# A two-layer decoder trunk in float32: values kept in PSUM banks and worked on in place, the softmax divided on ScalarE, other chain rates

## The chip, the core and the metric

The kernel runs on one NeuronCore of a Trainium2 chip. The metric is the device time of one execution in microseconds (us), as the median of several runs: before the change 2885.41 us over three runs (2882.80, 2885.41 and 2891.74).

Five engines work side by side, each through its own instructions in order: TensorE (PE in the profile; its weight loads are PEld), VectorE (DVE), ScalarE (ACT), GpSimd (POOL) and SyncE (SP, which here only issues DMAs). Matmuls read SBUF and write PSUM banks of 128 x 512 float32 values. VectorE and ScalarE read and write both SBUF and PSUM; GpSimd works on SBUF here.

## The reference, cut to what matters

Sequence 1024, width 1024, two layers. `rmsnorm`, `layernorm` and `silu` are the usual ones.

```
for i in range(2):
    a = rmsnorm(h);  u = a @ w_in[i]                    # 2128 columns, split among:
    # q, k, v (8 heads of 64, 2 kv heads), indexer qi (16 heads of 64), ki, wi, conv input, pool input
    idx = sum over 16 heads of relu(qi_h . ki) * wi_h    # causal; the 256 largest keys per query are kept
    y_attn = softmax(q . k / 8 over the kept keys) @ v
    y_conv = silu(layernorm(causal depthwise conv of width 31 (a * sigmoid(g)))) @ conv_pw
    y_pool = (trailing means over 2/4/8/16 positions - x) @ pool_w * pool_scale
    h = h + rmsnorm(concat(y_attn, y_conv, y_pool) @ w_out[i])
    h = h + rmsnorm(square(relu(rmsnorm(h) @ w_up[i])) @ w_down[i])      # 1024 -> 4096 -> 1024
    h = h + sigmoid(h @ ple_gate[i]) * (p[i] @ ple_proj[i])
```

## The kernel before, in words

**Tiles.** Activations are kept transposed (channels on partitions) and the sequence is cut into two halves of 512 positions. Every dense product is a sum of three matmuls of 128 x 512: both operands are split into a high and a low part of a shorter format, and high x high, high x low and low x high are added in one PSUM bank (`dense`, lines L243 to L249). One *unit* (`unit`) is one output tile of 128 x 512 from eight input tiles: 24 matmuls. Its weights are split on the fly in `prepare`: ScalarE makes the high part (L204, `whi`), GpSimd the low part (L205, `wlo`), twice per unit. `split` (L260, L261) and `split_g` (L265, L266) split activations: ScalarE writes the high part, VectorE the difference.

**Stages.** `PHASES` names eight stages of (layer, half). A `win` stage runs the 21 units of the `w_in` product (names M0, M1, MK, I0 to I7, V, Q0 to Q2 for the attention part, A, G, P for convolution and pooling); an `m` stage runs the 8 units of `w_out`, a norm with part of the per-layer embedding, 64 units of up and down projection, a second norm and the 8 units of the gate. By the DMAs of the weights they start at these times of the trace: `win` of layer 0 at 2.1 us (both halves, one behind the other), `m` of layer 0, first half, at 307.1; `win` of layer 1, first half, at 976.2; `m` of layer 0, second half, at 1124.2; `win` of layer 1, second half, at 1647.3; `m` of layer 1, first half, at 1785.4; `m` of layer 1, second half, at 2395.3 up to the end.

**The chain.** Convolution, pooling and attention of a (layer, half) form a second stream of work, written as generators (`conv_pool`, `attention`). Attention has four parts: `index` (scores of 16 heads, ReLU, weighted sum), `select` (the 256th largest value by bisection, 31 passes of counting, then the ties), `softmax` and `weighted` (transposes and the product with v). Each generator yields an estimate of its own cost. `run` puts it between the units: after each unit the chain may spend the unit's cost times the stage's rate in `RATES`. `drain` runs what is left of a (layer, half) before its `m` stage. So `RATES` decides beside which units each part of the chain stands; the order of the instructions on each engine is then made by the scheduler of the tile framework from this program.

**Buffers.** PSUM has 8 banks here: three of ring `pd` for the units and five of ring `bank` for the chain. `dtmp`, `row`, `ctmp`, `cmat` and `slot` are SBUF tiles. `yT` is the running output tile row in SBUF, `rb` the norm factor. A bank is taken when a product is begun (`pd.get`, `banks.get`) and can be written again when the last instruction that reads it has ended (`put`).

**What is touched.** `Sq.add` (L279, L283) squares a tile on ScalarE into a `dtmp` tile and adds it to a sum on VectorE; `evac` (L341) multiplies a bank by `rb` into a `dtmp` tile, which `put` then splits and stores; `index` (L632, L636, L638) evaluates ReLU from a bank into an SBUF row and adds the weighted row; `softmax` (L759 to L769) adds the mask and takes the maximum, exponentiates on ScalarE, and divides on VectorE; the up projection (L969, L971) and the gate (L1006, L1008, L1010) work on `dtmp` tiles.

## Time and profile before

| | us |
|---|---|
| median of three runs | 2885.41 |
| lowest, highest run | 2882.80, 2891.74 |
| the profiled execution | 2882.24 |
| its span, first to last instruction | 2880.4 |
| TensorE busy | 2736.7 (95%) |
| TensorE weight loads | 2250.3 (78%) |
| VectorE busy | 1917.1 (67%) |
| ScalarE busy | 1477.3 (51%) |
| GpSimd busy | 1468.7 (51%) |
| TensorE clock granted, mean over the span | 0.980 |

Busy time is the share of the span in which an engine has an instruction in work. Matmuls overlap in TensorE's pipeline, so the sum of their durations is larger than its busy time. The granted clock is given as a share of full speed: 1.00 is 2.4 GHz, 0.50 is 1.2 GHz, and other values are means over stretches at the two levels. The span can be cut into stretches (a view by windows); a wait is idle time of an engine that ended when another engine's instruction ended, and it is put down to that one.

### The profile page before, as it was taken

How to read it: one execution, taken by the hardware profiler on the slowest of the kernel's cores; microseconds unless marked ns; L12 is line 12 of the kernel's file. 1: busy time of each engine (PE TensorE's matmuls, PEld its weight loads, DVE VectorE, ACT ScalarE, POOL GpSimd, SP SyncE). 2: the span in 40 equal slices, each digit the busy share in tenths (PEclk: the TensorE clock that was granted, in tenths of full speed). 3: DMA queues.
4: the chain of work that ended last, by engine and by line, in shares of the span. 5: the costliest groups of instructions: out<-in, count | busy, mean ns of one | idle time of the engine just before them, and what ended most of it. 6: DMA issues, size and time to landing. Idle time of an engine off the chain costs nothing.

```text
span 2880.4 us, 37724 instructions
## 1 busy us (share of the span) xinstructions
PE 2736.7 (95%) x12648; PEld 2250.3 (78%) x12648; DVE 1917.1 (67%) x3473; ACT 1477.3 (51%) x2804; POOL 1468.7 (51%) x1161
## 2 busy tenths in 40 slices
PE   7889999999998899999999989999999999999998
PEld 6677877787887677778888767878878878788886
DVE  7989779899768877896312558699996662511123
ACT  5356567774553423675434423677744644533343
POOL 4655435444333766554444775455443346544446
PEclk9999999999998999999999999999999999999999
DMA  5676564332433456633323457544223344432233
GB/s 186 194 194 204 161 154 115 100 101 85 103 94 119 158 160 214 187 116 106 98 98 113 136 181 224 149 123 114 93 87 98 104 147 153 147 103 95 95 110 124
DMA packets 195667, 384.91 MB, mean 134 GB/s; under 512 B 17424, under 2 KB 76944, under 8 KB 195472
## 3 DMA queue, kind: packets, MB, share of 16 engines
q1 hardware_dynamic: 138192, 330.58, 35.1%
q0 software_dynamic: 57280, 51.91, 8.7%
q8 instruction: 100, 1.64, 0.2%
q14 instruction: 95, 0.78, 0.1%
HBM read 307.97 MB, written 74.45 MB: 133 GB/s over the span
## 4 chain that ended last, share of the span: by engine, by line
PE 68%; DVE 17%; DMA 6%; issue 4%; POOL 2%; ACT 2%; SPq 0%; POOLq 0%; ACTq 0%; DVEq 0%
PE pd L243 19%; PE pd L249 19%; PE pd L248 19%; PE bank L591 5%; DVE bank L527 3%; PE bank L781 2%; DVE idx L638 2%; POOL wlo L205 1%; DVE dtmp L261 1%; PE bank L790 1%; PE bank L789 1%; DVE slot L266 1%; DMA wraw<-win 1%; DVE dtmp L867 1%; DMA row<-cpS 1%
## 5 line engine op out<-in xcount | busy, mean ns | idle before, releaser
L205 POOL TENSOR_TENSOR wlo<-wraw,whi 128x512 fp32r<-128x512 f32 x824 | 1130.8, 1378 | 1151.0 <-ACT whi L204 1101.2
L243 PE MATMUL pd<-slot,whi 128*128 128x512 f32 x3296 | 1310.4, 398 | 55.3 <-ACT slot L260 11.5
L248 PE MATMUL pd<-slot,whi 128*128 128x512 f32 x3168 | 1248.1, 394 | 4.3 <-DVE slot L266 3.2
L249 PE MATMUL pd<-slot,wlo 128*128 128x512 f32 x3168 | 1242.6, 394 | 3.7 <-POOL wlo L205 3.4
L204 ACT ACTIVATE whi<-wraw 128x512 fp32r<-128x512 f32 x824 | 511.1, 627 | 717.0 <-PE pd L248 494.1
L243 PEld LDWEIGHTS pd<-slot,whi 128*128 128x128 f32 x3296 | 628.4, 191 | 197.1 <-ACT whi L204 18.8
L249 PEld LDWEIGHTS pd<-slot,wlo 128*128 128x128 f32 x3168 | 601.0, 190 | 129.7 <-POOL wlo L205 7.8
L248 PEld LDWEIGHTS pd<-slot,whi 128*128 128x128 f32 x3168 | 602.0, 190 | 126.7 <-DVE slot L266 5.8
L591 PE MATMUL bank<-kd,qst 128*128 128x512 f32 (+3 forms) x1024 | 249.2, 362 | 24.4 <-DVE mxc L759 10.9
L591 PEld LDWEIGHTS bank<-kd,qst 128*128 128x128 f32 x1024 | 181.6, 193 | 57.5 <-DVE mxc L759 12.8
L969 DVE SCALAR_TENSOR_TENSOR dtmp<-pd,rb 128x512 f32<-128x512 f32 x112 | 76.8, 686 | 199.9 <-PE pd L249 199.9
L985 DVE TENSOR_TENSOR yT<-yT,pd 128x512 f32<-128x512 f32 x96 | 65.7, 685 | 197.2 <-PE pd L249 196.9
L638 DVE SCALAR_TENSOR_TENSOR idx<-row,wiT,idx 128x640 f32<-128x640 f32 (+3 forms) x120 | 164.2, 1369 | 20.0 <-ACT row L632 16.0
L261 DVE TENSOR_TENSOR slot<-dtmp,slot 128x512 fp32r<-128x512 f32 x144 | 118.2, 825 | 72.5 <-ACT slot L260 72.2
L527 DVE SCALAR_TENSOR_TENSOR bank<-row,vec,bank 128x512 f32<-128x512 f32 x232 | 163.4, 745 | 0.6
L632 ACT ACTIVATE row<-bank 128x512 f32<-128x512 f32 (+3 forms) x256 | 120.4, 522 | 51.0 <-PE bank L591 39.0
L661 DVE TENSOR_SCALAR_CACHE_REDUCE row<-row,cc 128x640 f32<-128x640 uint16 (+1 forms) x124 | 133.6, 1077 | 16.5 <-ACT row L675 14.6
L283 DVE TENSOR_TENSOR dtmp<-dtmp,dtmp 128x512 f32<-128x512 f32 x100 | 105.0, 1050 | 50.5 <-ACT dtmp L279 49.5
L675 ACT ACTIVATE row<-row,cc 128x768 f32<-128x768 uint16 (+1 forms) x124 | 121.6, 983 | 25.2 <-DVE cc L681 17.5
L971 ACT ACTIVATE dtmp<-dtmp 128x512 f32<-128x512 f32 x128 | 80.1, 629 | 86.6 <-DVE dtmp L969 84.5
L261 DVE TENSOR_TENSOR cmat<-bank,cmat 128x512 fp32r<-128x512 f32 (+1 forms) x160 | 98.3, 630 | 31.1 <-ACT cmat L260 22.3
L759 DVE CUSTOM_DVE_ANT_0 row<-bank,idx 128x512 f32<-128x512 f32 (+3 forms) x160 | 90.8, 591 | 33.1 <-PE bank L591 28.6
(211 smaller groups left out, 2925.0 us busy)
## 6 DMA issues: line engine op xcount, KB each, us to landing
wraw<-wup SPq DMA_DIRECT2D x128, 512.0 KB, 3.2
wraw<-wdown SPq DMA_DIRECT2D x128, 512.0 KB, 3.2
wraw<-win SPq DMA_DIRECT2D x84, 512.0 KB, 4.1
qiS<-dtmp SPq DMA_DIRECT2D x64, 256.0 KB, 2.5
slot<-mixS POOLq DMA_DIRECT2D x32, 512.0 KB, 7.6
wraw<-wgate SPq DMA_DIRECT2D x32, 512.0 KB, 3.4
qst<-qiS POOLq DMA_DIRECT2D x48, 256.0 KB, 4.4
hS<-yT SPq DMA_DIRECT2D x48, 256.0 KB, 2.4
```

Source lines behind the costliest of these rows:

```text
L204: sc.activation(hi, r, AF.Copy)
L205: gp.tensor_tensor(lo, r, hi.bitcast(F32), op=OP.subtract)
L243: te.matmul(ps, wh, xh, start=i == 0, stop=False)
L248: te.matmul(ps, wh, xl, start=False, stop=False)
L249: te.matmul(ps, wl, xh, start=False, stop=i == n - 1)
L261: ve.tensor_tensor(lo, src, hi.bitcast(F32), op=OP.subtract)
L527: ve.scalar_tensor_tensor(acc[:, c] if k == TAPS - 1 else pa, src, w, pa, op0=OP.mult, op1=OP.add)
L591: te.matmul(ps[:, :n1 - n0], q, kd[:, k, k0 + n0:k0 + n1], start=k == 0, stop=k == 1)
L632: sc.activation(r[:, n0:n1], ps[:, :n1 - n0], AF.Relu)
L638: ve.scalar_tensor_tensor(idx[j], r, w, idx[j], op0=OP.mult, op1=OP.add)
L661: ve.tensor_scalar(flags[:, :Ws[j]], of[j], t, None, op0=op, op1=OP.add, accum_out=dst[:, j:j + 1])
L675: sc.activation(flags[:, :Ws[j]], of[j], AF.Sign, scale=-1.0, bias=c[:, j:j + 1], accum_out=cnt[:, j:j + 1])
```

## The change

Six edits, and one table of numbers:

- `Sq.add` takes a bank: the square is written into the bank in place of a `dtmp` tile, except where the tile is kept (the first, and the last where `apart`). In `m` stages the callers hand over the unit's own bank; where the row of `yT` is copied out of it, that copy now stands ahead of the square.
- `scaled` multiplies a bank by `rb` in place, for MK, I2 to I7, Q0 to Q2 and the G columns; `put` then splits out of the bank, which is given back after the split.
- In `index`, ReLU is done in place in the bank, and VectorE adds each piece of up to 512 columns from its bank: two instructions for a head of more than 512 keys, where one stood.
- In `softmax`, ScalarE multiplies by the reciprocal (a Copy with a scale per partition) where VectorE did.
- In the up projection ReLU and norm factor, square and split work in the bank; in the gate, tanh works in the bank and the product with the embedding is written over the embedding's tile.
- `put` no longer gives the source tile back; its callers do.
- `RATES` has other values for six of the eight stages.

```diff
--- before
+++ after
@@ -34,3 +34,3 @@
 
-RATES = (1.2, 1.193, 0.65, 0.823, 0.722, 0.567, 0.768, 0.919)
+RATES = (1.171, 1.114, 0.558, 0.766, 0.722, 0.567, 0.741, 0.946)
 
@@ -276,6 +276,8 @@
 
-        def add(self, src):
-            s = dtmp.get()
+        def add(self, src, bank=None):
+
+            keep = self.n == 0 or self.apart and self.n == NK - 1
+            s = dtmp.get() if keep or bank is None else bank
             sc.activation(s, src, AF.Square)
-            if self.n == 0 or self.apart and self.n == NK - 1:
+            if keep:
                 self.acc.append(s)
@@ -283,3 +285,4 @@
                 ve.tensor_tensor(self.acc[0], self.acc[0], s, op=OP.add)
-                dtmp.put(s)
+                if bank is None:
+                    dtmp.put(s)
             self.n += 1
@@ -343,2 +346,7 @@
 
+        def scaled(ps):
+
+            ve.tensor_tensor(ps, ps, rb, op=OP.mult)
+            return ps
+
         def put(x, parts):
@@ -350,3 +358,3 @@
                     sy.dma_start(dst[k, r0:r0 + b - a, ts], y[a:b])
-            dtmp.put(hi, lo, x)
+            dtmp.put(hi, lo)
 
@@ -379,3 +387,3 @@
                 c = int(name[1])
-                g = evac(ps)
+                g = scaled(ps)
                 sc.activation(g, g, AF.Tanh, scale=0.5)
@@ -384,3 +392,3 @@
                 sy.dma_start(cpS[l, c * P:(c + 1) * P, ts], y)
-                dtmp.put(g, y)
+                dtmp.put(y)
             elif kind == "P":
@@ -409,2 +417,3 @@
                 put(e, [(96, 112, kS[l], 176)])
+                dtmp.put(a, d, e)
             elif name == "I1":
@@ -413,6 +422,7 @@
                 put(d, [(0, P, qiS, P)])
+                dtmp.put(a, d)
             elif name == "MK":
-                put(evac(ps), [(0, P, kS[l], 48)])
+                put(scaled(ps), [(0, P, kS[l], 48)])
             elif kind == "I":
-                put(evac(ps), [(0, P, qiS, P * int(name[1]))])
+                put(scaled(ps), [(0, P, qiS, P * int(name[1]))])
                 if name == "I7":
@@ -420,3 +430,3 @@
             elif kind == "Q":
-                put(evac(ps), [(0, P, qS, P + P * int(name[1]))])
+                put(scaled(ps), [(0, P, qS, P + P * int(name[1]))])
                 if name == "Q2":
@@ -628,13 +638,11 @@
                         q = load_q(qiS, b, h, 16)
-                    t = spare.get()
-                    r = t[:, :W]
+                    w = wiT[:, l, b, h:h + 1]
                     for n0, n1, ps in scores(q[:, h % 4], W, 0):
-                        sc.activation(r[:, n0:n1], ps[:, :n1 - n0], AF.Relu)
+                        r, at = ps[:, :n1 - n0], idx[j][:, n0:n1]
+                        sc.activation(r, r, AF.Relu)
+                        if h == 0:
+                            ve.tensor_scalar(at, r, w, None, op0=OP.mult)
+                        else:
+                            ve.scalar_tensor_tensor(at, r, w, at, op0=OP.mult, op1=OP.add)
                         banks.put(ps)
-                    w = wiT[:, l, b, h:h + 1]
-                    if h == 0:
-                        ve.tensor_scalar(idx[j], r, w, None, op0=OP.mult)
-                    else:
-                        ve.scalar_tensor_tensor(idx[j], r, w, idx[j], op0=OP.mult, op1=OP.add)
-                    spare.put(t)
                     if h % 4 == 3:
@@ -768,3 +776,3 @@
                 ve.reciprocal(ri, rs)
-                ve.tensor_scalar(s, s, ri, None, op0=OP.mult)
+                sc.activation(s, s, AF.Copy, scale=ri)
                 out.append(t)
@@ -939,7 +947,7 @@
                 ve.tensor_tensor(yT[:, o], yT[:, o], ps, op=OP.add)
-                sq.add(yT[:, o])
+                sq.add(yT[:, o], ps)
             else:
                 ps = unit(xs)
-                sq.add(ps)
                 sc.activation(yT[:, o], ps, AF.Copy)
+                sq.add(ps, ps)
             pd.put(ps)
@@ -963,2 +971,3 @@
                     rb = rms_sb(sq)
+                m = slots.get()
                 if early:
@@ -966,10 +975,11 @@
                     ve.tensor_tensor(t, t, rb, op=OP.mult)
+                    sc.activation(t, t, AF.Square)
+                    split(m[:, 0], m[:, 1], t)
+                    dtmp.put(t)
                 else:
-                    ps, t = unit(xs), dtmp.get()
-                    ve.scalar_tensor_tensor(t, ps, 0.0, rb, op0=OP.max, op1=OP.mult)
+                    ps = unit(xs)
+                    ve.scalar_tensor_tensor(ps, ps, 0.0, rb, op0=OP.max, op1=OP.mult)
+                    sc.activation(ps, ps, AF.Square)
+                    split(m[:, 0], m[:, 1], ps)
                     pd.put(ps)
-                sc.activation(t, t, AF.Square)
-                m = slots.get()
-                split(m[:, 0], m[:, 1], t)
-                dtmp.put(t)
                 ms.append(m)
@@ -985,5 +995,5 @@
                     ve.tensor_tensor(yT[:, o], yT[:, o], ps, op=OP.add)
+                if gr == 3:
+                    sqy.add(yT[:, o], ps)
                 pd.put(ps)
-                if gr == 3:
-                    sqy.add(yT[:, o])
                 yield 5.2
@@ -1004,9 +1014,7 @@
             ps = unit(xs, o < 2)
-            th = dtmp.get()
-            sc.activation(th, ps, AF.Tanh, scale=0.5)
-            pd.put(ps)
-            ve.scalar_tensor_tensor(th, th, 1.0, e, op0=OP.add, op1=OP.mult)
+            sc.activation(ps, ps, AF.Tanh, scale=0.5)
+            ve.scalar_tensor_tensor(e, ps, 1.0, e, op0=OP.add, op1=OP.mult)
             y = yT[:, o]
-            gp.tensor_tensor(y, y, th, op=OP.add)
-            dtmp.put(e, th)
+            gp.tensor_tensor(y, y, e, op=OP.add)
+            dtmp.put(e)
             if last:
@@ -1015,3 +1023,3 @@
                 sy.dma_start(hS[o * P:(o + 1) * P, ts], y)
-                nsq.add(y)
+                nsq.add(y, ps)
                 if o == NK - 1:
@@ -1023,2 +1031,3 @@
                     split_g(x[:, 0], x[:, 1], yT[:, j], vec[:, l + 1, V_MIX_PRE + j:V_MIX_PRE + j + 1])
+            pd.put(ps)
             yield 6.5
```

On VectorE, while the index of layer 0, second half, is computed beside the first norm of the `m` stage (`idx_132` is the index of the seventh block of 128 queries, 896 keys wide; L283 and L285 add squares), before and now:

```order
L638 SCALAR_TENSOR_TENSOR idx_132<-row_127,wiT,idx_132 128x896
L283 TENSOR_TENSOR dtmp_104<-dtmp_104,dtmp_102 128x512
L638 SCALAR_TENSOR_TENSOR idx_132<-row_123,wiT,idx_132 128x896
L283 TENSOR_TENSOR dtmp_104<-dtmp_104,dtmp_101 128x512
L638 SCALAR_TENSOR_TENSOR idx_132<-row_125,wiT,idx_132 128x896
L283 TENSOR_TENSOR dtmp_104<-dtmp_104,dtmp_105 128x512
L638 SCALAR_TENSOR_TENSOR idx_132<-row_126,wiT,idx_132 128x896
```

```order
L646 SCALAR_TENSOR_TENSOR idx_132<-bank_141,wiT,idx_132 128x512
L285 TENSOR_TENSOR dtmp_109<-dtmp_109,dtmp_103 128x512
L646 SCALAR_TENSOR_TENSOR idx_132<-bank_144,wiT,idx_132 128x384
L285 TENSOR_TENSOR dtmp_109<-dtmp_109,dtmp_102 128x512
L646 SCALAR_TENSOR_TENSOR idx_132<-bank_143,wiT,idx_132 128x512
L646 SCALAR_TENSOR_TENSOR idx_132<-bank_140,wiT,idx_132 128x384
L646 SCALAR_TENSOR_TENSOR idx_132<-bank_142,wiT,idx_132 128x512
L646 SCALAR_TENSOR_TENSOR idx_132<-bank_141,wiT,idx_132 128x384
```

A head of 896 keys was one instruction that read an SBUF row; it is now a piece of 512 and a piece of 384, each out of a bank. The additions of squares between them come from `post_norm`, which hands no bank to `Sq.add`; they stay as they were.

On VectorE at the gate of layer 0, first half (L1008 and L1016 are the gate's product with the embedding), before and now:

```order
L527 SCALAR_TENSOR_TENSOR bank_143<-row_125,vec,bank_143 128x512
L1008 SCALAR_TENSOR_TENSOR dtmp_104<-dtmp_104,dtmp_108 128x512
L527 SCALAR_TENSOR_TENSOR bank_140<-row_125,vec,bank_140 128x512
L527 SCALAR_TENSOR_TENSOR bank_143<-row_125,vec,bank_143 128x512
L1008 SCALAR_TENSOR_TENSOR dtmp_102<-dtmp_102,dtmp_110 128x512
L527 SCALAR_TENSOR_TENSOR bank_140<-row_125,vec,bank_140 128x512
L527 SCALAR_TENSOR_TENSOR bank_143<-row_125,vec,bank_143 128x512
L527 SCALAR_TENSOR_TENSOR bank_140<-row_125,vec,bank_140 128x512
L266 SCALAR_TENSOR_TENSOR slot_79<-yT,vec,slot_79 128x512
```

```order
L767 ISA row_127,mxc_1404<-bank_140,idx_133 128x512
L767 ISA mxc_1404 128x1
L771 TENSOR_SCALAR nmc_1408<-mxc_1404 128x1
L1016 SCALAR_TENSOR_TENSOR dtmp_103<-pd_137,dtmp_103 128x512
L776 RECIPROCAL ric_1416<-rsc_1412 128x1
L1016 SCALAR_TENSOR_TENSOR dtmp_102<-pd_138,dtmp_102 128x512
L261 TENSOR_TENSOR cmat_122<-bank_141,cmat_121 128x512
L261 TENSOR_TENSOR cmat_118<-bank_144,cmat_117 128x512
L261 TENSOR_TENSOR cmat_120<-bank_143,cmat_119 128x512
```

The taps of the second half's convolution (L527) stood between the gate's instructions; now the last heads of that half's attention stand there (L767 mask and maximum, L776 reciprocal, L261 with `cmat` the split of transposed weights), and the convolution comes later, beside the next `win` stage.

On VectorE in the down projections of layer 0, second half (L985 and L995 add a unit to `yT`), before and now:

```order
L985 TENSOR_TENSOR yT<-yT,pd_137 128x512
L985 TENSOR_TENSOR yT<-yT,pd_138 128x512
L985 TENSOR_TENSOR yT<-yT,pd_139 128x512
L985 TENSOR_TENSOR yT<-yT,pd_137 128x512
L985 TENSOR_TENSOR yT<-yT,pd_138 128x512
L985 TENSOR_TENSOR yT<-yT,pd_139 128x512
```

```order
L537 SCALAR_TENSOR_TENSOR bank_144<-row_123,vec,bank_144 128x512
L537 SCALAR_TENSOR_TENSOR bank_143<-row_123,vec,bank_143 128x512
L509 TENSOR_TENSOR ctmp_116<-row_127,row_126 64x16 x2
L537 SCALAR_TENSOR_TENSOR bank_144<-row_123,vec,bank_144 128x512
L995 TENSOR_TENSOR yT<-yT,pd_139 128x512
L537 SCALAR_TENSOR_TENSOR bank_143<-row_123,vec,bank_143 128x512
L537 SCALAR_TENSOR_TENSOR bank_144<-row_123,vec,bank_144 128x512
L261 TENSOR_TENSOR cmat_120<-ctmp_116,cmat_119 128x512
L537 SCALAR_TENSOR_TENSOR bank_143<-row_123,vec,bank_143 128x512
L537 SCALAR_TENSOR_TENSOR bank_144<-row_123,vec,bank_144 128x512
L266 SCALAR_TENSOR_TENSOR ctmp_115<-bank_140,vec,ctmp_114 128x512
```

The convolution of layer 1, first half (L537 taps, L510 pooling), which stood in the `win` stage of its own layer, now stands here, among units that had nothing of the chain beside them.

## Rows read from the trace of the kernel before

**Rows 1.** The page: the span, and busy time, share and instructions of each engine.

```profile
span 2880.4 us, 37724 instructions
...
PE 2736.7 (95%) x12648; PEld 2250.3 (78%) x12648; DVE 1917.1 (67%) x3473; ACT 1477.3 (51%) x2804; POOL 1468.7 (51%) x1161
```

**Rows 2.** View by windows: stretch, its length, busy time of each engine, granted clock.

```profile
core 0: us, PE busy (x) PEld busy (x) DVE busy (x) ACT busy (x) POOL busy (x), PEclk, DMA share, GB/s
54.00:144.00 90.00, 76.23 (x315) 60.19 (x314) 87.64 (x118) 32.18 (x55) 55.42 (x43) 0.95 0.62 196
432.00:516.00 84.00, 78.11 (x350) 63.15 (x348) 83.38 (x78) 58.86 (x116) 48.40 (x35) 1.00 0.48 119
640.00:684.00 44.00, 37.38 (x157) 30.50 (x156) 43.16 (x66) 16.43 (x31) 19.02 (x14) 0.92 0.26 84
897.00:1010.00 113.00, 95.84 (x389) 74.37 (x387) 97.94 (x122) 41.54 (x73) 66.20 (x51) 0.86 0.46 146
1036.00:1124.00 88.00, 77.69 (x327) 61.32 (x326) 81.53 (x110) 25.57 (x45) 56.60 (x45) 0.94 0.62 198
1368.00:1512.00 144.00, 144.00 (x665) 120.02 (x665) 40.70 (x79) 55.04 (x95) 63.34 (x50) 1.00 0.30 98
1584.00:1656.00 72.00, 68.62 (x304) 54.36 (x303) 41.55 (x41) 32.52 (x57) 51.00 (x35) 1.00 0.41 137
1656.00:1785.00 129.00, 114.92 (x489) 91.33 (x487) 95.07 (x117) 39.02 (x68) 82.33 (x67) 0.96 0.65 201
1872.00:1926.00 54.00, 47.84 (x223) 38.72 (x222) 52.30 (x47) 39.28 (x80) 31.51 (x23) 1.00 0.47 139
2096.00:2142.00 46.00, 41.58 (x183) 33.85 (x182) 45.05 (x70) 17.94 (x34) 20.62 (x14) 0.96 0.27 86
2304.00:2376.00 72.00, 66.34 (x341) 55.23 (x340) 43.67 (x75) 32.09 (x56) 35.01 (x29) 0.95 0.47 147
```

**Rows 3.** By source line: duration in ns, least, median and most, of two forms.

```profile
L283 DVE TENSOR_TENSOR dtmp<-dtmp,dtmp x100: 674/990/2978, 10.0 to 2811.8; 128x512 f32<-128x512 f32 x100
...
L985 DVE TENSOR_TENSOR yT<-yT,pd x96: 671/686/690, 620.2 to 2815.9; 128x512 f32<-128x512 f32 x96
```

**Rows 4.** Groups of VectorE by form: count, busy us, mean ns, idle before, releaser.

```profile
L261 DVE TENSOR_TENSOR slot<-dtmp,slot 128x512 fp32r<-128x512 f32 x144 | 118.2, 825 | 72.5 <-ACT slot L260 72.2
L283 DVE TENSOR_TENSOR dtmp<-dtmp,dtmp 128x512 f32<-128x512 f32 x100 | 105.0, 1050 | 50.5 <-ACT dtmp L279 49.5
...
L867 DVE SCALAR_TENSOR_TENSOR dtmp<-yT,vec,pd 128x512 f32<-128x512 f32 x64 | 46.6, 738 | 16.9 <-PE pd L300 13.8 <-POOL yT L868 2.9
L261 DVE TENSOR_TENSOR dtmp<-dtmp,dtmp 128x512 fp32r<-128x512 f32 x48 | 44.9, 938 | 2.4 <-ACT dtmp L260 2.3
...
L1008 DVE SCALAR_TENSOR_TENSOR dtmp<-dtmp,dtmp 128x512 f32<-128x512 f32 x32 | 38.7, 1212 | 54.8 <-ACT dtmp L1006 54.8
...
L759 DVE CUSTOM_DVE_ANT_0 row<-bank,idx 128x128 f32<-128x128 f32 x16 | 4.5, 283 | 3.6 <-PE bank L591 3.6
```

**Rows 5.** Groups by line, forms together: the index's sums, the softmax on both engines.

```profile
L638 DVE SCALAR_TENSOR_TENSOR idx<-row,wiT,idx 128x640 f32<-128x640 f32 (+3 forms) x120 | 164.2, 1369 | 20.0 <-ACT row L632 16.0
...
L767 ACT ACTIVATE row<-row,nmc 128x384 f32<-128x384 f32 (+5 forms) x96 | 84.3, 878 | 41.4 <-DVE nmc L763 34.1 <-DVE nmc L765 6.9
...
L769 DVE TENSOR_SCALAR row<-row,ric 128x384 f32<-128x384 f32 (+5 forms) x96 | 67.7, 706 | 2.8
...
L638 DVE SCALAR_TENSOR_TENSOR idx<-idx,wiT,idx 128x384 f32<-128x384 f32 (+1 forms) x60 | 54.8, 913 | 14.9 <-ACT idx L632 10.7 <-DVE idx L638 0.5
...
L769 DVE TENSOR_SCALAR ctmp<-ctmp,ric 128x128 f32<-128x128 f32 (+1 forms) x32 | 13.1, 413 | 0.2
```

**Rows 6.** Waits of TensorE from 640 to 684 us: total, times, longest.

```profile
PE bank L591 <- DVE mxc L759: 6.6, 1, 6.6
```

**Rows 7.** Timeline of ScalarE and VectorE at the gate: start, us, instruction, idle before.

```profile
1645.06 0.58 ACT L1006 ACTIVATE dtmp<-pd 128x512 f32<-128x512 f32 x1
...
1651.97 1.10 DVE L283 TENSOR_TENSOR dtmp<-dtmp,dtmp 128x512 f32<-128x512 f32 x1 [1.84 <-ACT dtmp L279]
```

## The prediction

> **What bounds the kernel now.** The page comes first [rows 1]: TensorE is busy for 2736.7 of 2880.4 us, so 143.7 us is all the time in which it does nothing, and no other engine is busy for more than 67% of the span. The view by windows comes second [rows 2]: it shows where those 143.7 us lie. In stretches with little beside the units TensorE is never idle: in 1368 to 1512 it is busy for 144.00 of 144.00 us at a granted clock of 1.00, while VectorE works for 40.70 us. It idles where VectorE is full: 13.77 us of 90 with VectorE busy for 87.64, 17.16 of 113 with 97.94, 5.89 of 84 with 83.38. In most of these stretches the granted clock is below 1.00 as well; a mean of 0.86 over 113 us is 15.8 us of full-speed time that TensorE did not get, because after an idle time part of the stretch ran at 1.2 GHz and not at 2.4. I call idle time plus that deficit the *pot* of a stretch: it is what the stretch could give back at the most.
>
> | stretch | what stands there | idle + deficit = pot, us |
> |---|---|---|
> | 54-144, 1036-1124, 1656-1785 | `win` stages with a convolution | 18.3 + 15.6 + 19.2 = 53.1 |
> | 897-1010 | second norm and gate of layer 0, first half, with a convolution | 17.2 + 15.8 = 33.0 |
> | 640-684, 2096-2142 | end of `select`, first scores after it | 10.1 + 6.3 = 16.4 |
> | 432-516, 1872-1926 | index of the wide blocks beside the first norm | 5.9 + 6.2 = 12.1 |
>
> The third view is by line [rows 3, 4]. A VectorE operation on two SBUF tiles of 512 columns takes 674 ns at the least, 990 in the median and up to 2978 (L283), and 1050 in the mean; with one operand in PSUM it takes 671 to 690 ns, every time (L985). So a PSUM operand buys no faster best case: it takes away a spread that comes only with two SBUF operands.
>
> **VectorE's work, part by part.** I price an operation with a PSUM operand at 686 ns [rows 3]; with a scale per partition at 738, as L867 has it [rows 4]; and narrow pieces by the line from 686 at 512 columns to 283 at 128 (L759), with the same 52 ns on top.
> - Squares: `Sq.add` with a bank covers 24 additions after `w_out`, 24 after the last down projection and 12 at the gates: 60 x (1050 - 686) = 21.8 us. The other 40 have no bank and stay.
> - Up projection: 112 subtractions 825 to 686: 15.6 us. Stored columns of the `win` stages: 40 subtractions 938 to 686: 10.1 us. Gate: 32 products 1212 to 686: 16.8 us.
> - Softmax: 67.7 + 13.1 = 80.8 us leave VectorE [rows 5]. ScalarE gets as many Copies; their form is not in the trace, and the exponentials of the same shapes (878 ns x 96 = 84.3 us for the long rows) bound them from above at about 100 us in all, 0 from below. ScalarE is busy for 51%, so I cost this at nothing where units fill TensorE; where a chain tail is run without cover, each head's division takes up to 0.17 us longer (878 against 706 ns).
> - Index: 180 instructions took 164.2 + 54.8 = 219.0 us [rows 5]. Now each width is cut at 512: the six widths cost 604, 738, 1073, 1207, 1342 and 1476 ns, times 30 = 193 us, a gain of 26. It is all in the widest blocks and in those that were held up; blocks of 640 and 768 keys gain nothing.
>
> Sum: 21.8 + 15.6 + 10.1 + 16.8 + 80.8 + 26 = 171 us of VectorE's 1917, 9%. Most of that lies where TensorE waits for nobody, so it isn't the answer; the pots are.
>
> [...]
>
> **What of it lies on the path.**
> - *Gate, 897-1010.* VectorE's order shows the convolution gone from here. What remains is like 1584-1656, the same place without a chain (pot 3.4), or like 2304-2376, the same place with an attention tail beside it (5.7 + 3.6 = 9.3) [rows 2], and about 5 us for the start of the next `win` stage. The order puts an attention tail there, so about 14 of 33.0 remain: 19 gained, bounds 6 and 25.
> - *Win stages, 53.1.* Each has ten stored columns whose subtraction gets 0.25 us shorter while VectorE is full: about 2.5 us each. Against it a `pd` bank is now held until after the split, at least 0.58 us of ScalarE and 0.69 of VectorE more [rows 3, 7], and three banks turn. Net 7 gained, bounds -7 and 15.
> - *End of select, 16.4.* TensorE's one wait of 6.6 us for the first masked maximum [rows 6] is a queue of tie-breaking work on VectorE that isn't touched; only what stands between it gets lighter. 4 gained, bounds -8 and 12.
> - *Index beside the norm, 12.1.* Half of the waits there are for the norm itself, which isn't touched. 5 gained, bounds -4 and 9.
>
> Against these 35 us stand four costs, with the cover that each has:
> - The convolution of layer 1, first half, moves in among down projections where TensorE had no idle time at all [rows 2]. VectorE has 103 of 144 us free there, enough for 62 taps at 738 ns (46 us), so the taps cost nothing; its small dense products and token sums must still wait for their splits on an in-order TensorE. 3 us, bounds 0 and 10.
> - Banks held longer at the gate. In the trace the way from tanh to the added square is 1645.06 to 1653.07, 8.0 us [rows 7]; the bank is now held over all of it, where 0.6 us did. Two units on the other two banks cover 10.4 us (2 x 24 matmuls at 144.00 us / 665 = 0.217 us, [rows 2]). It is hidden with 2 us to spare; 2 us for the units that come in pairs, bounds 0 and 16 (1 us for each of 16).
> - The last square after `w_out` now follows the copy of the same bank: 0.6 us at each of three norms, 2 us.
> - The lower rates of `m` stages let an attention tail reach into a norm or a gate: 2 us, bounds 0 and 8.
>
> Sum: 19 + 7 + 4 + 5 - 3 - 2 - 2 - 2 = 26 us. The profiled execution took 2882.2 us, 1.8 over its span; that is 3.2 under the median of the runs and inside their spread. 2882.2 - 26 = 2856.2, and on the footing of the median 2859.
>
> **The rivals.**
> - *Relief spreads.* With 171 us off VectorE its queue no longer runs late, TensorE doesn't fall idle, and the clock stays at 2.4 GHz: half of all pots (114.6 us) come back with no cost that shows, 57 us, so 2828. For it: the deficits are nearly as large as the idle times, and a stretch that never idles has none. Against it: several of these waits are for ScalarE, GpSimd or a norm's chain of small steps.
> - *The waits stay.* TensorE idles because its own order is fixed by the scheduler and each wait is a latency (split, norm, tie-breaking), not VectorE's load; what the gate gains is spent in the convolution's new place. 2885. For it: in 640-684 one wait of 6.6 us is two thirds of the pot. [...]
> - *Banks run out, slower.* In the index a bank was free after ReLU (about 0.6 us); now it waits for VectorE too, 0.74 us for its own piece and as much for the one before it. Wide heads take two banks each, so five banks hold two and a half heads, and TensorE's scores stand in order ahead of its units. Once VectorE is more than five pieces (3.7 us) late, each further piece holds up the units behind it. VectorE is busy for 83.38 of 84 us there [rows 2]. If half of the 256 wide pieces of both layers cost 0.35 us each, that is 45 us: 2904. Against it: 26 us less work in just that place, and no two SBUF operands to be held up.
>
> **How the numbers follow.** Forecast 45%, relief spreads 22%, waits stay 18%, banks run out 15%. Within 0.3% of 2885.4 (2876.8 to 2894.1) is what a measurement of this kernel can't tell from no change. The forecast's own range is 2838 to 2880; all but a fifteenth of it counts as faster. Faster: 0.42 + 0.22 + 0.03 of the third case, 0.67. Within: 0.03 + 0.14, 0.17 in all. Slower: 0.15 and a little of the third, 0.16. The range that holds 8 in 10 reaches from "relief spreads", less 14 us that the gate and the `win` stages have left to their upper bounds, 2814, to where "banks run out" begins, 2892.
>
> **What would show it.** Right: no L537 beside the gate of layer 0, first half, and a pot there below 20 us; additions of squares and subtractions at 670 to 690 ns without a tail; VectorE near 1750 us; TensorE's waits for `DVE` in the `win` stages shorter. Wrong: TensorE waits for VectorE's index rows (`idx`) at the scores, more than a few us in all, or for the squares at the gate; or idle time of TensorE above 143 us in all. If TensorE's idle time falls by far more than 26 us, the first rival is right; if it falls only in 897-1010, the second is close.

## The result, and the profile after

The changed kernel takes 2842.68 us (median of four runs, 2840.33 to 2843.85), the kernel before in the same session 2884.11: a ratio of 0.9854 with a 95% interval of 0.9829 to 0.9878, 41.4 us less. The forecast was 2859 with its own range of 2838 to 2880: the time lies in that range, 16 us below the forecast. The profiled execution took 2843.85 us. The page of after, span and busy time, against [rows 1]:

```profile
span 2842.1 us, 37724 instructions
...
PE 2720.5 (96%) x12648; PEld 2242.8 (79%) x12648; DVE 1747.6 (61%) x3473; ACT 1548.1 (54%) x2932; POOL 1418.0 (50%) x1161
```

TensorE's idle time fell from 143.7 to 121.6 us, its mean granted clock rose from 0.980 to 0.985, which is a deficit of (1 - 0.985) x 2842 = 42.6 us in place of 57.6. Together that is 37 us of the 38.3 by which the span is shorter. So nearly all of the gain is idle time and clock, and the pots are the right thing to look at. They are bounds and not exact shares: idle time at a low clock counts twice in a pot, and since the view gives the clock in two digits, the pot of a stage of some 380 us is known to about 2 us. VectorE is busy for 169.5 us less; 171 were worked out.

The durations, after, by line and form (instruction, its operands, count | busy us, mean ns | idle before), against [rows 4, 5]; the first two are those of the source lines with least/median/most in ns, against [rows 3]:

```profile
L285 DVE TENSOR_TENSOR dtmp<-dtmp,pd x60: 672/686/689, 401.6 to 2773.0; 128x512 f32<-128x512 f32 x60
L285 DVE TENSOR_TENSOR dtmp<-dtmp,dtmp x40: 666/684/3155, 8.8 to 2442.5; 128x512 f32<-128x512 f32 x40
```

```profile
L261 DVE TENSOR_TENSOR slot<-pd,slot 128x512 fp32r<-128x512 f32 x112 | 76.6, 685 | 51.3 <-ACT slot L260 51.1
...
L261 DVE TENSOR_TENSOR dtmp<-pd,dtmp 128x512 fp32r<-128x512 f32 x40 | 27.3, 682 | 7.4 <-ACT dtmp L260 7.3
...
L1016 DVE SCALAR_TENSOR_TENSOR dtmp<-pd,dtmp 128x512 f32<-128x512 f32 x32 | 22.0, 690 | 64.8 <-ACT pd L1015 59.8 <-DMA outT<-yT 4.9
```

```profile
L646 DVE SCALAR_TENSOR_TENSOR idx<-bank,wiT,idx 128x512 f32<-128x512 f32 (+3 forms) x300 | 189.3, 652 | 94.7 <-ACT bank L642 90.7
```

```profile
L777 ACT ACTIVATE row<-row,ric 128x384 f32<-128x384 f32 (+5 forms) x96 | 83.1, 876 | 9.0 <-DVE ric L776 8.9
...
L777 ACT ACTIVATE ctmp<-ctmp,ric 128x128 f32<-128x128 f32 (+1 forms) x32 | 14.1, 447 | 7.3 <-DVE ric L776 6.4 <-DVE nmc L773 0.9
```

Every edited addition and subtraction stands at 682 to 690 ns; the same line with two SBUF operands still has a tail up to 3155. The trace shows what stands beside the long ones: rows of GpSimd. Here is that longest addition, with the GpSimd rows beside it, and then an addition out of PSUM with one beside it (start us, duration, instruction):

```profile
1866.55 3.15 DVE L285 TENSOR_TENSOR dtmp<-dtmp,dtmp 128x512 f32<-128x512 f32 x1
1866.60 2.55 POOL L205 TENSOR_TENSOR wlo<-wraw,whi 128x512 fp32r<-128x512 f32 x2
...
930.40 0.69 DVE L285 TENSOR_TENSOR dtmp<-dtmp,pd 128x512 f32<-128x512 f32 x1 [0.32 <-ACT pd L281]
930.02 1.30 POOL L205 TENSOR_TENSOR wlo<-wraw,whi 128x512 fp32r<-128x512 f32 x1 [0.56 <-ACT whi L204]
```

Of the 100 additions of L283 in before, the 28 with no GpSimd row beside them took 674 to 692 ns; the 72 with one took 676 to 2978, with a median of 1100. Of the 60 out of PSUM in after, 50 had one, and they took 676 to 689 ns.

The index takes 189.3 us (193 worked out), the division costs ScalarE 97.2 us (bound: about 100).

Where the time came from is read by stage. These are windows of before, cut at the DMAs of the stages' first weights (columns as in [rows 2]): second norm and gate of layer 0, first half; `win` of layer 1, first half; then of layer 0, second half, `w_out` up to the DMA of the first down projection's weights (the first up projections run then), and the rest up to its second norm.

```profile
891.30:976.20 84.90, 72.55 (x278) 55.24 (x277) 79.34 (x109) 32.56 (x57) 46.52 (x35) 0.86 0.39 122
976.20:1124.20 148.00, 132.21 (x582) 106.50 (x582) 120.86 (x150) 47.41 (x83) 96.71 (x78) 0.94 0.60 192
1124.20:1257.40 133.20, 125.24 (x600) 103.78 (x599) 106.38 (x254) 84.67 (x186) 74.46 (x65) 0.99 0.62 174
1257.40:1582.20 324.80, 324.80 (x1503) 270.90 (x1502) 139.62 (x328) 154.21 (x291) 150.97 (x118) 1.00 0.33 105
```

The same four of after:

```profile
852.40:934.00 81.60, 81.07 (x437) 68.75 (x436) 58.11 (x132) 60.67 (x105) 41.45 (x32) 1.00 0.37 115
934.00:1070.00 136.00, 132.45 (x640) 109.67 (x639) 99.47 (x141) 53.42 (x93) 88.85 (x76) 1.00 0.66 197
1070.00:1208.60 138.60, 128.82 (x593) 105.85 (x592) 101.59 (x278) 91.91 (x212) 71.57 (x64) 0.96 0.61 176
1208.60:1549.20 340.60, 334.61 (x1540) 277.78 (x1539) 181.60 (x362) 164.37 (x310) 158.86 (x127) 0.99 0.35 109
```

At the gate TensorE now idles 0.53 us, not 12.35, at a clock of 1.00, not 0.86; in the `win` stage behind it 3.55, not 15.79. The lengths say less than the losses: more of the chain's matmuls stand at this gate now (x437 for x278), so it is only 3 us shorter. Idle plus clock deficit (the *pot*) of each kind of stage, worked out from such windows in us (l0 h0 is layer 0, first half; `mid` is everything from that DMA to the second norm, with the end of `select` in it; the last stage, layer 1 second half, is 16.2 and 17.2):

| stage | before | after | rates alone | places alone | before, 58 taps out | up projection in SBUF |
|---|---|---|---|---|---|---|
| `win` layer 0, both halves | 47.7 | 50.0 | 51.7 | 46.7 | 48.7 | 52.5 |
| `w_out`, norm: l0 h0 | 17.8 | 17.5 | 19.7 | 18.2 | 20.5 | 18.9 |
| mid l0 h0 | 13.9 | 10.8 | 11.6 | 9.6 | 13.5 | 4.2 |
| gate l0 h0 | 24.2 | 0.5 | 1.7 | 22.2 | 10.9 | 0.6 |
| `win` l1 h0 | 24.7 | 3.6 | 5.3 | 11.4 | 15.2 | 4.3 |
| `w_out`, norm: l0 h1 | 9.3 | 15.3 | 15.2 | 8.4 | 16.1 | 14.5 |
| mid l0 h1 | 0.0 | 9.4 | 1.4 | 7.0 | 1.3 | 2.7 |
| gate l0 h1 | 3.4 | 4.8 | 3.4 | 4.8 | 3.3 | 3.9 |
| `win` l1 h1 | 19.6 | 18.7 | 18.1 | 16.8 | 20.5 | 17.4 |
| `w_out`, norm: l1 h0 | 6.7 | 3.2 | 7.1 | 2.5 | 6.7 | 2.4 |
| mid l1 h0 | 4.4 | 6.9 | 7.7 | 6.7 | 10.3 | 10.4 |
| gate l1 h0 | 8.8 | 4.7 | 5.9 | 10.6 | 7.8 | 3.9 |
| all, with the last stage | 196.7 | 162.5 | 165.0 | 180.8 | 190.6 | 151.3 |

Two neighbouring stages, gate l0 h0 and `win` l1 h0, give 44.8 us; 15.4 of it go back in the two stages behind them. The second of these losses, 9.4 us in mid l0 h1, is for the most part one new wait. Waits of TensorE (total us, times, longest) in that stage of after, 1208.6 to 1549.2 us:

```profile
PE pd L243 <- DVE slot L261: 3.4, 1, 3.4
```

The clock falls in this wait, to 0.50 from 1219.5 to 1226.2 us, and costs as much again (0.99 over 340.60 us, 3.4 us). In the whole span of after:

```profile
PE pd L243 <- DVE slot L261: 14.5, 6, 4.3
...
PE bank L601 <- DVE mxc L767: 3.7, 4, 1.7
```

The first kind does not occur in before; the second does:

```profile
PE bank L591 <- DVE mxc L759: 10.9, 2, 6.6
```

L243 begins a unit; what it waits for is the `pd` bank that the split of an up projection (L261, `slot<-pd,slot`) still reads. The longest of the six, in mid l0 h0, on VectorE (start us, duration, instruction):

```profile
680.21 1.57 DVE L755 TENSOR_SCALAR idx<-idx 128x640 f32<-128x640 f32 x1
681.70 3.08 DVE L752 TENSOR_TENSOR_SCAN row<-row 128x896 f32<-128x896 f32 x1
684.70 0.66 DVE L261 TENSOR_TENSOR slot<-pd,slot 128x512 fp32r<-128x512 f32 x1
```

and on TensorE:

```profile
685.41 0.79 PE L243 MATMUL pd<-slot,whi 128*128 128x512 f32 x1 [4.29 <-DVE slot L261]
686.00 0.63 PE L248 MATMUL pd<-slot,whi 128*128 128x512 f32 x1
686.43 0.63 PE L249 MATMUL pd<-slot,wlo 128*128 128x512 f32 x1
686.86 0.63 PE L243 MATMUL pd<-slot,whi 128*128 128x512 f32 x1
```

The subtraction, 0.66 us long, stands behind tie-breaking rows of 1.57 and 3.08 us; TensorE waits 4.29 us for it, and then starts its matmuls 0.427 us apart at a granted clock of 0.50, where ahead of the wait they stood 0.226 apart at 1.00. At half the clock that is 512 columns / 0.427 us = 1.2 a ns, and so, as an estimate, 2.4 at the whole: read the GHz of the text ahead as these. The matmuls at 1.00 came to 512 / 0.226 = 2.27; 0.217 us [rows 2] is a mean with narrower ones in it. The 6.60 us behind the wait have a granted clock of 0.62 (columns as in [rows 2]):

```profile
676.00:681.00 5.00, 5.00 (x23) 3.90 (x21) 5.00 (x6) 2.64 (x5) 2.90 (x2) 1.00 0.14 57
684.00:690.00 6.00, 4.59 (x11) 3.62 (x12) 6.00 (x10) 0.53 (x2) 0.00 (x0) 0.50 0.04 16
685.40:692.00 6.60, 6.59 (x19) 5.22 (x20) 6.60 (x11) 1.76 (x4) 1.34 (x1) 0.62 0.00 0
```

### The profile page after: what moved, and what is told of

Read it like the earlier page. It is cut to its first block, busy times and chain, and to the rows that moved or that the text cites. A ratio compares the mean times of both kernels' runs of the same rounds, so it can differ in the third digit from the quotient of the medians.

```text
span 2842.1 us, 37724 instructions
## 1 busy us (share of the span) xinstructions
PE 2720.5 (96%) x12648; PEld 2242.8 (79%) x12648; DVE 1747.6 (61%) x3473; ACT 1548.1 (54%) x2932; POOL 1418.0 (50%) x1161
## 4 chain that ended last, share of the span: by engine, by line
PE 72%; DVE 16%; DMA 5%; ACT 3%; issue 3%; POOL 1%; SPq 0%; POOLq 0%; DVEq 0%; ACTq 0%
PE pd L243 20%; PE pd L249 20%; PE pd L248 20%; PE bank L601 5%; DVE bank L537 2%; PE bank L789 2%; DVE dtmp L875 1%; DVE row L669 1%; DVE slot L261 1%; DMA row<-cpS 1%; PE bank L798 1%; PE bank L797 1%; DVE cmat L261 1%; PE pd L298 1%; DVE dtmp L261 1%
## 5 line engine op out<-in xcount | busy, mean ns | idle before, releaser
L205 POOL TENSOR_TENSOR wlo<-wraw,whi 128x512 fp32r<-128x512 f32 x824 | 1094.7, 1334 | 1180.6 <-ACT whi L204 1115.4
L243 PE MATMUL pd<-slot,whi 128*128 128x512 f32 x3296 | 1306.8, 397 | 50.7 <-DVE slot L261 14.5
L248 PE MATMUL pd<-slot,whi 128*128 128x512 f32 x3168 | 1246.0, 393 | 4.6 <-DVE slot L261 2.7
L243 PEld LDWEIGHTS pd<-slot,whi 128*128 128x128 f32 x3296 | 625.6, 190 | 188.4 <-DVE slot L261 16.6
L248 PEld LDWEIGHTS pd<-slot,whi 128*128 128x128 f32 x3168 | 601.1, 190 | 125.8 <-DVE slot L266 3.9
L601 PE MATMUL bank<-kd,qst 128*128 128x512 f32 (+3 forms) x1024 | 261.5, 360 | 10.6 <-DVE mxc L767 3.7
L646 DVE SCALAR_TENSOR_TENSOR idx<-bank,wiT,idx 128x512 f32<-128x512 f32 (+3 forms) x300 | 189.3, 652 | 94.7 <-ACT bank L642 90.7
L642 ACT ACTIVATE bank<-bank 128x512 f32<-128x512 f32 (+2 forms) x320 | 153.8, 506 | 90.0 <-PE bank L601 85.2
L981 DVE SCALAR_TENSOR_TENSOR pd<-pd,rb 128x512 f32<-128x512 f32 x112 | 77.7, 694 | 183.2 <-PE pd L249 183.2
L995 DVE TENSOR_TENSOR yT<-yT,pd 128x512 f32<-128x512 f32 x96 | 65.5, 684 | 197.8 <-PE pd L249 197.5
L537 DVE SCALAR_TENSOR_TENSOR bank<-row,vec,bank 128x512 f32<-128x512 f32 x232 | 162.1, 746 | 0.5
L669 DVE TENSOR_SCALAR_CACHE_REDUCE row<-row,cc 128x640 f32<-128x640 uint16 (+1 forms) x124 | 133.5, 1077 | 14.5 <-ACT row L683 12.6
L683 ACT ACTIVATE row<-row,cc 128x768 f32<-128x768 uint16 (+1 forms) x124 | 121.5, 983 | 18.0 <-DVE cc L689 15.3
L767 DVE CUSTOM_DVE_ANT_0 row<-bank,idx 128x512 f32<-128x512 f32 (+3 forms) x160 | 91.4, 591 | 64.0 <-PE bank L601 60.6
L261 DVE TENSOR_TENSOR cmat<-bank,cmat 128x512 fp32r<-128x512 f32 (+1 forms) x160 | 97.9, 631 | 49.4 <-ACT cmat L260 43.8
L261 DVE TENSOR_TENSOR slot<-pd,slot 128x512 fp32r<-128x512 f32 x112 | 76.6, 685 | 51.3 <-ACT slot L260 51.1
L982 ACT ACTIVATE pd<-pd 128x512 f32<-128x512 f32 x112 | 65.2, 582 | 72.8 <-DVE pd L981 72.7
L775 ACT ACTIVATE row<-row,nmc 128x384 f32<-128x384 f32 (+5 forms) x96 | 84.2, 878 | 27.8 <-DVE nmc L771 21.0
```

The source lines that it names most:

```text
L205: gp.tensor_tensor(lo, r, hi.bitcast(F32), op=OP.subtract)
L243: te.matmul(ps, wh, xh, start=i == 0, stop=False)
L248: te.matmul(ps, wh, xl, start=False, stop=False)
L261: ve.tensor_tensor(lo, src, hi.bitcast(F32), op=OP.subtract)
L537: ve.scalar_tensor_tensor(acc[:, c] if k == TAPS - 1 else pa, src, w, pa, op0=OP.mult, op1=OP.add)
L601: te.matmul(ps[:, :n1 - n0], q, kd[:, k, k0 + n0:k0 + n1], start=k == 0, stop=k == 1)
```

## The experiments

Each kernel was timed against the kernel before in its own session (2881.7 to 2882.9 us). Distances between two other kernels are those of their medians. The kernel before took 1 to 2 us more in the session of the changed kernel (2884.11), so distances from the changed kernel are open by about as much.

**Which half of the change pays.** The kernel before with the new `RATES` alone, and the changed kernel with the old `RATES`.

```
rates_alone   -RATES = (1.2, 1.193, 0.65, 0.823, 0.722, 0.567, 0.768, 0.919)       in the kernel before
              +RATES = (1.171, 1.114, 0.558, 0.766, 0.722, 0.567, 0.741, 0.946)
places_alone  the same two lines exchanged                                         in the changed kernel
```

> The kernel before with the new RATES alone. Theory P (where the chain stands is what counts: no convolution beside the gate of layer 0, first half): most of the gain, 2853 to 2866 us, and the stretch of the gate without a low clock. Theory V (VectorE's 171 us less work is what counts): the rates alone give nothing, since the chain is as heavy as before: 2876 to 2895.

> The changed kernel with the old RATES: in-place work and division on ScalarE, the convolution again beside the gate of layer 0, first half. Theory P: a third of the gain or less, 2865 to 2880. Theory V: most of the gain, 2843 to 2860.

Measured: 2851.13 us, ratio 0.9890 (0.9877 to 0.9904), and 2863.75, 0.9936 (0.9922 to 0.9949). The numbers in `RATES` bring 30.7 us without one edit of a tile, 2 us more than theory P's range, and VectorE's busy time is then what it was (1916.5 us). The places bring 18.1 where they are alone, which lies between the ranges of the two theories, and 8.5 on top of the rates: the two overlap. Either alone takes more than half of the pot of the `win` stage l1 h0 (24.7 to 5.3, to 11.4).

**Is it the convolution at the gate?** The kernel before, with 58 of VectorE's 62 taps left out of the convolution that stands there (layer 0, second half), so that this part isn't computed.

```diff
-                else:
+                elif (l, hf) != (0, 1) or k == TAPS - 1:
                     ve.scalar_tensor_tensor(acc[:, c] if k == TAPS - 1 else pa, src, w, pa, op0=OP.mult, op1=OP.add)
```

> The kernel before, with 58 of the 62 taps that VectorE runs left out of the convolution of layer 0, second half (the one that stands beside the gate of the first half); the rest of that pass stays, so this part of the result is not computed. Theory P (the pot of 33.0 us at 897-1010 us is VectorE working on the convolution and the gate at once, and the change empties it by moving the convolution away): the loss of that stretch falls to 14 us or less and the time is 2855 to 2866. Rival (the gate waits for its own norm and for ScalarE, whatever stands beside it): at least 10 us of that fall is missing and the time is 2876 or more.

Measured: 2877.60 us, ratio 0.9986 (0.9978 to 0.9994). In its trace the four stages, and 897 to 1010 us, are:

```profile
894.40:973.30 78.90, 71.19 (x319) 56.85 (x318) 59.52 (x70) 37.85 (x66) 51.55 (x38) 0.96 0.44 146
973.30:1108.70 135.40, 124.31 (x538) 99.07 (x536) 101.77 (x130) 42.36 (x74) 91.11 (x74) 0.97 0.63 202
1108.70:1246.10 137.40, 126.79 (x594) 104.73 (x594) 99.86 (x230) 81.37 (x175) 73.04 (x65) 0.96 0.62 169
1246.10:1573.90 327.80, 326.53 (x1509) 271.39 (x1507) 144.13 (x354) 157.09 (x302) 149.97 (x118) 1.00 0.33 104
897.00:1010.00 113.00, 102.10 (x458) 81.04 (x457) 75.12 (x82) 50.64 (x89) 80.94 (x62) 0.97 0.54 180
```

On the place theory P is nearly right: the first two stages together are 18.6 us shorter (214.3 for 232.9), and the pot in 897 to 1010 is 10.9 + 3.4 = 14.3, not 33.0 [rows 2], where P had 14 or less. On the time it is wrong, and the rival's number holds without its mechanism: 6.8 us go back in the next `w_out` stage, 5.9 in the mid stage of l1 h0, and the execution had lost 3 us before it came to the edit. Why the later stages lose more was not found. The `win` stage l1 h0 has its own 60 taps as before and still gained 9.5 us of pot: what VectorE is late by at the gate is carried into the stage behind it, as rows. The end of the first convolution's pass (from L541 on) stood inside that stage in before, and stands beside the norm here; before, then this kernel:

```profile
997.55 0.15 DVE L541 TENSOR_SCALAR muc<-bank 128x4 f32<-128x4 f32 x1
```

```profile
915.87 0.15 DVE L541 TENSOR_SCALAR muc<-bank 128x4 f32<-128x4 f32 x1
```

The taps explain 22.8 us of pot in the two stages; the new rates take 41.9 from them. What the rest hangs on (the other rows of that pass, its sums and splits, which stayed here) was not separated.

**What the bank is held for.** The up projection's product with the norm factor goes to an SBUF tile again, in all 112 units or (second kernel) only in those that are issued while `select` runs (39 of 112 by the trace).

```diff
-                    ps = unit(xs)
-                    ve.scalar_tensor_tensor(ps, ps, 0.0, rb, op0=OP.max, op1=OP.mult)
-                    sc.activation(ps, ps, AF.Square)
-                    split(m[:, 0], m[:, 1], ps)
+                    ps, t = unit(xs), dtmp.get()
+                    ve.scalar_tensor_tensor(t, ps, 0.0, rb, op0=OP.max, op1=OP.mult)
                     pd.put(ps)
+                    sc.activation(t, t, AF.Square)
+                    split(m[:, 0], m[:, 1], t)
+                    dtmp.put(t)
```

> The changed kernel with the up projection worked on in SBUF again (bank given back after VectorE's first instruction). Theory H (the longer hold of a pd bank costs, since its last reader stands behind tie-breaking rows on VectorE): TensorE's waits for L261 with slot, 17.2 us in all in the changed kernel, go away with their low clock: 2824 to 2836. Rival (the 15.6 us that VectorE saves there count): 2843 to 2855, waits for VectorE elsewhere.

> The changed kernel, where the up projection's last addition goes to an SBUF tile for the units that are issued while the select chain runs (40 of 112), and stays in the bank elsewhere. Theory H (the loss of the up projection in the bank is the hold of the pair bank behind the chain's long rows on VectorE, in the select alone): as good as with all of them in SBUF, 2826 to 2838, and PE no longer waits for the sum row (slot) in the select. Rival (the hold costs nothing there, the gain came from elsewhere): 2840 to 2850, like the changed kernel.

Measured: 2833.83 us, 0.9831 (0.9818 to 0.9844), and 2835.68, 0.9837 (0.9825 to 0.9850). Both are where theory H has them. In neither is there a wait of L243 for `slot` L261 any more. From 580 to 700 us, where after has four of them (7.1 us in all), the second kernel has:

```profile
PE pd L243 <- DVE nmc L773: 1.9, 1, 1.9
PE pd L243 <- DVE dtmp L985: 1.1, 1, 1.1
PE pd L249 <- POOL wlo L205: 0.2, 1, 0.2
```

The three mid stages have pots of 17.3 us together in both kernels, against 27.1 in after: about the difference in time. A part goes to the scores' wait for the masked maximum (9.0 and 9.6 us for 3.7). These are the fastest kernels of the study; their intervals overlap with that of the changed kernel (0.9829 to 0.9878), so that they beat it is likely and not certain. Giving the bank back early doesn't always help, either. In the kernel before with the new rates alone, where the up projection works in SBUF throughout, TensorE has two waits for the bank's first reader on VectorE (L969; 4.1 and 3.5 us, both in mid stages), so that one can be late too:

```profile
PE pd L243 <- DVE dtmp L969: 7.7, 2, 4.1
```

**The other places, undone one at a time** in the changed kernel (the gate's product was not undone by itself): the stored columns of `win` through `evac` to SBUF, the division on VectorE, ReLU into an SBUF row and whole rows in the index, squares into SBUF.

```
win_in_sbuf       scaled(ps): return evac(ps); put() and the G columns give x and g back to dtmp
divide_on_vector  ve.tensor_scalar(s, s, ri, None, op0=OP.mult)      for  sc.activation(s, s, AF.Copy, scale=ri)
index_in_sbuf     sc.activation(r[:, n0:n1], ps[:, :n1 - n0], AF.Relu); banks.put(ps); one sum over the whole r
squares_in_sbuf   bank = None; s = dtmp.get()                        in Sq.add
```

> The changed kernel with the stored and the G columns of the win stages worked on in SBUF again. Theory H: TensorE's waits for L261 with dtmp, 9.5 us in the changed kernel, go down to some 5 for the first instruction (L344): 2834 to 2842. Rival (VectorE is full there, each subtraction 0.25 us longer counts): 2847 to 2855.

> The changed kernel with the softmax divided on VectorE again (81 us more on VectorE, as much less on ScalarE). Theory P: most of it is hidden behind units, 2842 to 2850. Theory V: it is the largest single part of the relief, half of the gain goes, 2855 to 2868.

> The changed kernel with the index's ReLU written to an SBUF row again, one sum per head (26 us more on VectorE). Theory P: 2842 to 2848. Theory V: 2850 to 2860, with waits in the two stretches of the index beside the first norm. Banks that are held too long in the changed kernel would show as a faster one here: 2832 to 2840.

> The changed kernel with the squares in SBUF tiles again, banks given back as before the change's hand-over (21.8 us more on VectorE, additions again held up by GpSimd). Theory P: 2840 to 2848. Theory V: 2848 to 2856, at the gates above all.

Measured, with the distance from the changed kernel's 2842.7: 2858.50 us (+15.8), 2852.85 (+10.2), 2859.96 (+17.3), 2844.89 (+2.2); ratios 0.9922, 0.9893, 0.9923 and 0.9869, each with 0.0013 to 0.0015 either way. The columns cost more than either range, the index what theory V says, the division lies between the theories, the squares cost what P says. The profiled execution of the columns' kernel was 9 us above its median, so its trace overstates the loss. With the up projection's -8.9 these five sum to +36.6 us. Yet undoing all places at once, the gate's too (`rates_alone`), costs only 8.5. Prices of single edits don't add here.

**How far is a neutral reorder?** All eight rates of the changed kernel times 0.99; and two of the undone edits at once.

```
rates_nudged        RATES = (1.159, 1.103, 0.552, 0.758, 0.715, 0.561, 0.734, 0.937)
up_squares_in_sbuf  the edits of up_in_sbuf and squares_in_sbuf together
```

> The changed kernel with all eight rates of the chain times 0.99, no other edit: the same work, each unit of it a place or two earlier or later among the dense work. If what lies next to what by a place or two is worth little, 2838 to 2850 (within 0.3% of the changed kernel). If single stretches hang on the exact neighbours, the time leaves that by 10 us or more to one side, and differences of 10 us between the other kernels of this study can't be read as the price of the edit alone.

> The changed kernel with two of its edits undone: the up projection's last addition goes to an SBUF tile again (as in the run that gave 2833.8 us) and the squares of the norms are copied to SBUF again (2844.9 us alone, against 2842.7). Theory H (the first gives 9 us because the pair bank comes back at the first row, the second is nearly worth nothing): 2828 to 2840. Rival (the gain of the first hung on the order of that kernel): 2842 to 2855.

Measured: 2851.93 us, 0.9893 (0.9879 to 0.9908), and 2850.85, 0.9891 (0.9878 to 0.9904). One per cent on the rates moves the time by 9 us, out of the band for a harmless order and as much as some of the edits. The second is outside theory H: the mid stages lose 27.4 us, as in after, though no L243 waits for `slot` L261 there; other waits for VectorE stand in the mid stages in its place (the masked maximum `mxc` 4.9 us, `yT` 3.2, the split at L248 3.9). So the squares cost 2.2 us in one kernel and 17.0 in the other, and the order alone can make some 15 us. Of the distances between single edits only that of `four_pd` below is well above this; `win_in_sbuf` (15.8) and `index_in_sbuf` (17.3) are not, and for them, as for the others, it is the waits in the trace that say something of the edit. So of three kernels with the up projection in SBUF two are 7 to 9 us faster than after and one is 8 slower. The wait and the queue that it stands in are shown; that its removal is worth 9 us holds only for the order that it was tried in.

**A fourth `pd` bank** (four for units, four for the chain).

```diff
-    pd = Ring("pd", 3, [P, HALF], pool=psum)
-    banks = Ring("bank", 5, [P, HALF], pool=psum)
+    pd = Ring("pd", 4, [P, HALF], pool=psum)
+    banks = Ring("bank", 4, [P, HALF], pool=psum)
```

> The changed kernel with four pd banks and four for the chain in place of three and five. Theory H: TensorE's waits for pd readers (L261 with slot 17.2 us, with dtmp 9.5 us) go to a few us, and waits at the chain's banks (L601, now 6.4 us for VectorE) grow: between 2828 and 2848. Rival (a bank more for units is of no use, and the chain needs its five): 2850 to 2875.

Measured: 2870.50 us, 0.9960 (0.9947 to 0.9973), 27.8 slower than after. The first stages gain (`win` of layer 0: pot 39.8 for 50.0), but `w_out` of l0 h0 goes from 17.5 to 42.9 and that of l1 h1 from 4.1 to 29.5, with one wait of 11.0 us for the attention's output. At these rates the chain needs its fifth bank more than the units a fourth.

## Why the prediction was right, and where its sizes were off

- *The bound and the sum on VectorE*: right. 169.5 us for 171, the edited rows at 682 to 690 ns where 686 was put; the tails went with the second SBUF operand. An addition with an operand in PSUM is typically no slower: the medians of L285 are 686 ns with one and 684 with two SBUF tiles. The tail with two SBUF operands, up to 3155 ns, has no like out of PSUM (757 at the most, L537), and it stood beside GpSimd's rows: of the 40 such additions of after, the 23 with no GpSimd row beside them took 666 to 694 ns, the 17 with one 675 to 3155. In SBUF the up projection came out better, in two kernels of three, but for the bank's sake and not for the instruction's.
- *Gate, 19 us*: mis-sized, and the largest miss. The step that failed is "about 14 of 33.0 remain": with the attention tail in the convolution's place 0.5 us remains at this gate and 3.6 in the whole `win` stage behind it. I took the `win` stage's pot for the load of its own columns and convolution; the run without taps shows that 9.5 of its 24.7 us came with the convolution at the gate, whose last rows ran into it. The two stages gave 44.8 us where 19 and a part of 7 were put. Taps beside the columns do not make a stage lose by themselves: in after, the `win` stage still has 60 of them (another half's, L537; VectorE's rows of that line alone) and loses 3.6:

```profile
934.00:1070.00 136.00, 41.66 (x60) 1.00 0.66 197
```

- *`win` stages, 7 us*: with `win` l1 h0 counted above, the two others give 0.9 and lose 2.3: nothing. The cost that was named is there: TensorE's waits for the bank's first reader (L341, 10.7 + 3.5 us in before) for the most part became waits for its last (L261 on `dtmp`, 9.5 us in after). The sign "waits for `DVE` in the `win` stages shorter" came in l1 h0 alone, which had it from the rates as well. Undoing the columns costs 9 us of pot in the three stages and 15.8 in time, less than twice what a neutral reorder makes, so the term's size stays open.
- *End of `select`, 4 us*: mis-sized and the mechanism missed. The waits for the masked maximum fell from 10.9 to 3.7 us in the span, the one of 6.6 [rows 6] among them, but 14.5 us of waits for `pd` came. In the `win` stages and at the gate I asked what a longer hold of a bank costs; in the up projection, where 112 of the units are, I did not, and priced the edit by its duration alone. The pots of mid l0 h0 and l1 h0 together went from 18.3 to 17.7, and mid l0 h1, which had none, has 9.4.
- *Index, 5 us*: 3.8 came in the two `w_out` stages of the first halves, but that is no proof of the term: the neutral nudge moves these two by 5.9 (26.6 for 20.7). With the index in SBUF again they lose 9.9 more than after, with the squares in SBUF 8.3. "Banks run out" did not happen: TensorE's waits for `idx` sum to 2.7 us.
- *Convolution among down projections, 3 us*: 1.4 in the kernel with the rates alone.
- *Banks held at the gate, 2 us*: the two gates with nothing else new lose 1.4 and 1.5 us more. The way from tanh to the added square, at the gate of layer 0, second half, answers to [rows 7]; ScalarE's row, then VectorE's:

```profile
1610.31 0.58 ACT L1015 ACTIVATE pd<-pd 128x512 f32<-128x512 f32 x1
```

```profile
1611.29 0.68 DVE L1016 SCALAR_TENSOR_TENSOR dtmp<-pd,dtmp 128x512 f32<-128x512 f32 x1
...
1614.44 0.69 DVE L285 TENSOR_TENSOR dtmp<-dtmp,pd 128x512 f32<-128x512 f32 x1 [2.47 <-ACT pd L281]
```

It takes 4.8 us now, not 8.0.
- *Square after the copy, 2 us; attention tails, 2 us*: neither shows. `w_out` l1 h0 and gate l1 h0 lose 3.5 and 4.1 us less than before.
- *Not foreseen*: `w_out` of l0 h1 loses 5 to 7 us more in each kernel that relieves the gate ahead of it (15.3, 15.2, 16.1, 14.5) and not with the places alone (8.4). What is late there was not settled; in after TensorE's waits there are for a split of the activations (L266, 3.9 us), the attention's output (2.2), the transposed weights (1.2) and others of 1 us or less.

"Relief spreads" was partly right: of 38 us 15 are clock. "The waits stay" is refuted by the gate; a part of it, that a gain is spent further on, is what the run without taps shows.

The mechanism at the gate was forecast and came; that the sum came so near is partly luck. The two emptied stages gave some 20 us more than was put, no other gain can be told from the noise of order, and 15.4 us that no term had went back in the stages behind.

## What to carry to other kernels

Find which stages idle, and ask whether the lateness was made there or carried in; a stage can be healed by what leaves the stage ahead. Price a value that stays in PSUM twice: by its instruction, and by the queue in which its readers stand, since the bank is held until the last of them has run (here six waits, 14.5 us). With two SBUF operands, look for GpSimd rows beside the instruction before you price it (L283: a median of 1100 ns with one, 692 at the most without). Where two streams are interleaved by a table of rates, try a neutral nudge of the table first: differences below what it makes are not prices of edits, and one nudge is one sample of what order can make.

## What was not expected of the hardware

A TensorE stop of 4.29 us cost more than its length: the matmuls behind it started 0.427 us apart, not 0.226, and a clock of 0.62 over 6.60 us is another 2.5 us. An addition of two SBUF tiles that met two GpSimd rows took 3.15 us: it ended 0.55 us after the second of them. ScalarE's square in place in a bank takes 582 ns (L982), where the SBUF tile took 629; its Copy with a scale per partition takes 876 ns, as the exponential of the same shapes does (878).
